# State-space layer of a decoder step: PSUM sums of prompt and samples parted, output powers formed with PSUM operands

## Chip, cores and metric

One core of one Trainium2 chip. The metric is the time of one execution on the device in microseconds (us), the median of the runs; lower is better. A program is also executed once under the hardware profiler, and all rows below come from that execution.

## What is computed

A step of a two-layer decoder on 1024 prompt tokens and 8 x 4 sample tokens, width 1024, all in float32. Only the first half of layer 0 matters here, a diagonal state-space layer (S5): 64 groups of 16 channels, each group driving 64 complex states.

```
ab = exp(dt*a)                       (complex, per group and state)
bu = einsum('blgc,gnc->blgn', u, bb) (u: normed input; bb: input matrix)
x[l] = ab*x[l-1] + bu[l]             (prompt from 0, samples from a given state)
y = Re(einsum('blgn,gcn->blgc', x, c)) + d*u
out = glu(gelu(y) @ w_glu);  also returned: the last x of prompt and samples
```

A GLU, an MLP, the shared K/V projection and layer 1 (window attention and MLP) follow. They are large matmuls and the change doesn't touch them.

## The kernel before

The method `ssm` works the state-space layer off in eight **parts** (`ft`) of 8 groups, 128 channels. Tokens are taken 8 at a time: 128 blocks of the prompt, and 8 columns for the samples. For a part:

- `s1_p` (GpSimd) forms input powers, `s1_PT` transposes them on TensorE; `s1_u` scales the input (ScalarE), `s1_U` transposes it into `U`, 136 columns used as sums: 128 prompt blocks and 8 samples. `s1_e` (GpSimd) forms the rotation table `E`.
- `s1_q` (VectorE, lines 500 to 511) forms the output powers `Q` = powers of ab times C: six instructions of 128 x 512 elements, four multiplies (L508, L509), then L510 and L511. `ap9` holds the powers of ab, `Cq` holds C, `dt0` and `dt1` are work space; all of them in SBUF. GpSimd's complex multiplies run through L409 to L414.
- `s2_S` (L551): 16 matmuls of 136 columns sum blocks into the PSUM tile `b_s`, prompt and samples together, four banks; ScalarE copies the sample columns out (L560).
- `s2_rot` (VectorE): part 0 turns the sums (L577 to L579), part 1 runs eight scans (L570), turns back and writes the states `H_` (L572 to L574). All of it reads or writes `b_s` in place.
- `s1_K` (TensorE, L533) forms the short convolution kernel in a PSUM bank, `s1_K2` (VectorE, L536, L537) takes it out, and a round trip through DRAM on the SP queue (`kdd`) lays it out as `T_`.
- `s3_y` (TensorE, L591, L595): the output, in two halves with `s1_K` between, then gelu (ScalarE, L597). `s3_zt` and `s3_zT` transpose it back, each group of transposes into an auxiliary bank that ScalarE copies out (L603, L607, L613, L617; also L550, L523, L527 for the other transposes).

A matmul of float32 is two or more instructions in the trace (two for each of L558's). PSUM has eight banks of 512 floats in a partition. `self.psum(aux=4,s=1)` (L622) shares them out: four auxiliary ones in rotation, and one `b_s` of four banks. A tile that is reused waits for the last user of the buffer; within a tile, too, waits go by the tile and not by its columns. Each engine works its queue off in the order of the program, and the order is the source's. One turn of the loop (`i`), with part i+1 summed, part i put out and part i+2 prepared:

```
if ok(i+1): s2_S(i+1)
if ok(i+2): s1_u(i+2)
if ok(i): s3_y(i,K)          # K is s1_K(i+1), between its halves
s2_rot(i+1,0); s1_K2(i+1); s2_h(i+1); s2_rot(i+1,1)
if ok(i+2): s1_bd(i+2); s1_q(i+2); s1_PT(i+2)
if ok(i): s3_zt(i)
if ok(i+2): s1_U(i+2)
if ok(i): s3_zT(i)
if ok(i+2): s1_e(i+2)
if ok(i+3): s1_p(i+3)
```

Behind the loop the banks are shared out anew for the GLU (`acc=3`), whose first matmuls take banks that `b_s` had.

Of the kernel before, what the change touches and what calls it, by code (L numbers as in the profile page):

```python
# [5 lines left out]
F=mybir.dt.float32; R=mybir.dt.float32r; I32=mybir.dt.int32  # L6
AF=mybir.ActivationFunctionType; OP=mybir.AluOpType
P=128; D=1024; NT=1056; NB=352; KT=8; DFF=4096; EPS=1e-6
# [38 lines left out]
class Core:  # L47
# [212 lines left out]
    def ssm(self, out_p, out_s, early):  # L260
# [6 lines left out]
        def pc(t,a,n): return t[:,a:a+n]  # L267
        v3=lambda ap,g: ap.rearrange("p (g n) -> p g n",g=g)
        E_=[pc(S[i],0,1024).rearrange("p (c g k) -> p c g k",c=2,g=4) for i in (0,1)]
        U_=[v3(pc(S[i],1024,1152),8) for i in (0,1)]  # L270
        PT_=[v3(pc(S[i],0,1024),8) for i in (2,3)]
        Q_=[pc(S[i],1024,1152).rearrange("p (c g t e) -> p c g t e",c=2,g=4,t=9) for i in (2,3)]
        T_=[[W[0][:,0:848],W[6][:,0:848]],[S[i][:,0:848] for i in (4,5)]]
        H_=pc(S[4],1024,1096).rearrange("p (c g k) -> p c g k",c=2,g=4)
        dt0=pc(S[5],1024,576); dt1=pc(S[5],1600,576)
# [10 lines left out]
        Cq=pc(rt,1024,1024).rearrange("p (c g e) -> p c g e",c=2,g=32)  # L286
# [5 lines left out]
        Shi=pc(ex,576,512).rearrange("p (c b g) -> p c b g",c=2,b=8)  # L292
# [54 lines left out]
        pb=self.bank()  # L347
# [52 lines left out]
        sn=pc(W[6],0,256).rearrange("p (j g) -> p j g",j=8); cn=pc(W[6],256,256).rearrange("p (j g) -> p j g",j=8)  # L400
# [7 lines left out]
        def cmul(eng,o,a,b,t):  # L408
            eng.tensor_tensor(o[0],a[0],b[0],op=mult)  # L409
            eng.tensor_tensor(t[0],a[1],b[1],op=mult)  # L410
            eng.tensor_tensor(o[1],a[0],b[1],op=mult)
            eng.tensor_tensor(t[1],a[1],b[0],op=mult)
            eng.tensor_tensor(o[0],o[0],t[0],op=sub)
            eng.tensor_tensor(o[1],o[1],t[1],op=add)  # L414
# [37 lines left out]
        def xs_row(i):  # L452
            PL.tensor_tensor(xsb[i].rearrange("p g (r c) -> p r g c",r=8),xst[i].rearrange("p r (g c) -> p r g c",g=8),pc(W[3],800,8).unsqueeze(2).unsqueeze(3).to_broadcast([P,8,8,16]),op=mult)
# [8 lines left out]
        pb=self.bank()  # L462
# [17 lines left out]
            A.copy(pc(ac,1536,512),pb)  # L480
        kdd=self.dp.tile([8,16,1920],F,name="kdd")
        sh=[P,4,8,16]; sh7=[P,4,7,16]
        sp={}

        def gsl(ft): return slice(4*ft,4*ft+4)
        def s1_u(ft):
            for r in range(8):
                A.mul(uf[:,:,r,:],x_t[(7-r)//2][:,(7-r)%2,ft*128:ft*128+128].rearrange("p (g c) -> p g c",g=8),rp[:,7-r:8-r])
        def s1_p(ft,eng=PL,t=None):
            gs=gsl(ft); t=[a[:,0:448].rearrange("p (g t e) -> p g t e",g=4,t=7) for a in t or pt]  # L490
            A.copy(P_[:,:,:,0,:],Bg[:,:,gs,:])
            cmul(eng,[P_[:,0,:,1:8],P_[:,1,:,1:8]],[ap9[:,c,gs,1:8].unsqueeze(3).to_broadcast(sh7) for c in range(2)],
                 [Bg[:,c,gs,:].unsqueeze(2).to_broadcast(sh7) for c in range(2)],t)
        def s1_e(ft,eng=PL,t=None):
            gs=gsl(ft); t=[a[:,0:448].rearrange("p (g t e) -> p g t e",g=4,t=7) for a in t or pt]
            E=E_[ft%2]
            A.copy(E[:,:,:,0:16],B16[:,:,gs,:])
            cmul(eng,[E[:,c].rearrange("p g (t e) -> p g t e",e=16)[:,:,1:8] for c in range(2)],[A8[:,c,gs,1:8].unsqueeze(3).to_broadcast(sh7) for c in range(2)],
                 [B16[:,c,gs,:].unsqueeze(2).to_broadcast(sh7) for c in range(2)],t)
        def s1_q(ft):  # L500

            gs=gsl(ft); Q=Q_[ft%2]
            t0=dt0[:,0:512].rearrange("p (g t e) -> p g t e",g=4,t=8); t1=dt1[:,0:512].rearrange("p (g t e) -> p g t e",g=4,t=8)
            a=[ap9[:,c,gs,1:9].unsqueeze(3).to_broadcast(sh) for c in range(2)]
            q=[Cq[:,c,gs,:].unsqueeze(2).to_broadcast(sh) for c in range(2)]
            A.copy(Q[:,:,:,0,:],Cq[:,:,gs,:])
            q0,q1=Q[:,0,:,1:9],Q[:,1,:,1:9]
            V.tensor_tensor(q0,a[0],q[0],op=mult); V.tensor_tensor(t0,a[1],q[1],op=mult)  # L508
            V.tensor_tensor(q1,a[0],q[1],op=mult); V.tensor_tensor(t1,a[1],q[0],op=mult)  # L509
            V.tensor_tensor(q0,q0,t0,op=add)  # L510
            V.tensor_tensor(q1,q1,t1,op=sub)  # L511
# [4 lines left out]
        def s1_U(ft):  # L516
            U=U_[ft%2]
            for h in range(2):
                pb=self.bank()
                for i in range(4):  # L520
                    g=4*h+i
                    T.transpose(pb[:,i*128:i*128+128],uf[:,g,:,:],ident)
                A.copy(U[:,4*h:4*h+4,8:136],v3(pb,4))  # L523
            pb=self.bank(); p0=32*(ft%4)
            for g in range(8):
                T.transpose(pb[:,g*16:g*16+16],xsb[ft//4][p0:p0+16,g,:],ident[p0:p0+16,p0:p0+16])
            A.copy(U.rearrange("p g (a b) -> p g a b",b=8)[:,:,0:18:17,:],pb[:,0:128].rearrange("p (g a b) -> p g a b",g=8,a=2))  # L527
        kb={}
        def s1_K(ft):
            pb=kb[ft]=self.bank(); Q=Q_[ft%2]  # L530
            for gp in range(4):
                for c in range(2):
                    T.matmul(pb[32*gp:32*gp+32,0:128],Bd[ft%2][:,c,gp,:],Q[:,c,gp,0:8,:],start=c==0,stop=c==1)  # L533
# [8 lines left out]
        def s1_PT(ft):  # L542
            PT=PT_[ft%2]
            for h in range(2):
                pb=self.bank()
                pv=pb.rearrange("p (a g c n) -> p a g c n",a=2,g=2,c=2)
                for a in range(2):
                    for c in range(2):
                        T.transpose(pv[:,a,:,c,:],P_[:,c,2*h+a,:,:],ident)
                A.copy(PT[:,4*h:4*h+4,:],v3(pb,4))  # L550
        def s2_S(ft):  # L551

            PT=PT_[ft%2]; U=U_[ft%2]
            s=sp[ft]=self.pp["s"].tile([P,2,2,512],F,name="b_s",tag="b_s")
            for c in range(2):
                for gp in range(4):
                    for h in range(2):
                        T.matmul(s[64*h:64*h+64,c,gp//2,136*(gp%2):136*(gp%2)+136],PT[:,2*gp+h,64*c:64*c+64],U[:,2*gp+h,8:144],start=True,stop=True)  # L558
            for c in range(2):
                A.copy(Shi[:,c,:,gsl(ft)].rearrange("p q (b g) -> p b g q",b=2),s[:,c,:,0:272].rearrange("p b (g k) -> p b g k",g=2)[:,:,:,128:136])  # L560
        def s2_rot(ft,part):
            b4=lambda ap: ap.rearrange("p (b g) k -> p b g k",b=2)
            E=E_[ft%2]; Er,Ei=b4(E[:,0]),b4(E[:,1]); tt=V.tensor_tensor
            t0,t1=[t[:,0:512].rearrange("p (b g k) -> p b g k",b=2,g=2) for t in (dt0,dt1)]
            s=sp[ft]; Sr,Si=[s[:,c,:,0:272].rearrange("p b (g k) -> p b g k",g=2)[:,:,:,0:128] for c in range(2)]
            if part:
                for c in range(2):
                    for gp in range(4):
                        z=s[:,c,gp//2,136*(gp%2):136*(gp%2)+128]
                        V.tensor_tensor_scan(z,rho8[:,4*ft+gp:4*ft+gp+1].to_broadcast([P,128]),z,0.0,mult,add)  # L570
                Hr,Hi=[b4(H_[:,c,:,9:137]) for c in range(2)]
                tt(Hr,Sr,Er,op=mult); tt(Hi,Sr,Ei,op=mult)  # L572
                tt(Sr,Si,Ei,op=mult); tt(Si,Si,Er,op=mult)  # L573
                tt(Hr,Hr,Sr,op=sub); tt(Hi,Hi,Si,op=add)  # L574
                sp.pop(ft)
                return
            tt(t0,Si,Ei,op=mult); tt(t1,Sr,Ei,op=mult)  # L577
            tt(Sr,Sr,Er,op=mult); tt(Si,Si,Er,op=mult)
            tt(Sr,Sr,t0,op=add); tt(Si,Si,t1,op=sub)  # L579
# [39 lines left out]
        zl=self.zs=[]  # L619
        def split_z(n,eng=None):  # L620
            for k in range(len(zl),n): zl.append(self.xsplit(X[k],self.ZO[k],eng=eng))
        self.psum(aux=4,s=1)  # L622
        s1_p(0,V,[dt0,dt1]); s1_u(0); s1_q(0); s1_PT(0); s1_U(0); s1_e(0,V,[dt0,dt1]); s1_p(1); xs_row(1)
        for i in range(-1,7):
            if ok(i+1): s2_S(i+1)
# [27 lines left out]
        t=[pc(S[7],512+256*i,256).rearrange("p (b g) -> p b g",b=8) for i in range(2)]  # L653
# [566 lines left out]
```

## Time and profile before

| | |
|---|---|
| median of 3 runs (lowest, highest) | 2328.33 us (2324.35, 2329.13) |
| the profiled execution | 2328.08 us, its span 2326.3 us |
| busy: PE, PEld, DVE, ACT, POOL | 96%, 93%, 48%, 30%, 19% of the span |
| chain of work that ended last | PE 84%, DVE 11%, ACT 2%, issue 2%, POOL 1% |
| granted clock of TensorE, mean | 0.982 |

The profile names engines so: PE is TensorE's matmuls, PEld its weight loads, DVE is VectorE, ACT ScalarE, POOL GpSimd, SP the DMA queue. L157 is line 157 of the kernel. [...] The shares are means over the whole span, of which the state-space loop is less than a tenth, so they tell nothing of what binds it: that has to be read from the stretch itself.

### The profile page before, as it was taken

What the parts mean: (1) busy time and instruction counts of PE and PEld (TensorE: products, weight loads), DVE (VectorE), ACT (ScalarE), POOL (GpSimd) and SP (SyncE); (2) the same over time, 40 slices, a digit from 0 to 9 for tenths busy, and PEclk for the clock granted to TensorE, in tenths of its full rate; (3) what the DMA queues carried; (4) which work ended last, traced back from release to release, by engine and by line L of the source; (5) the groups of instructions that cost most, each with busy time, mean ns of one, the idle gap of its engine ahead of it and who ended that gap; (6) DMA issues with size and microseconds to landing.
All of it is one profiled execution on the core that took longest, in us unless ns stands there. A gap on an engine that the chain in (4) does not pass through costs nothing.

```text
span 2326.3 us, 35574 instructions
## 1 busy us (share of the span) xinstructions
PE 2231.5 (96%) x14614; PEld 2165.7 (93%) x14614; DVE 1111.9 (48%) x2271; ACT 702.7 (30%) x1496; POOL 439.0 (19%) x477
## 2 busy tenths in 40 slices
PE   4788999999999999999999899989999999999999
PEld 3667999999999999999999887779999999999998
DVE  8996232333333333333647788884333333333332
ACT  4456422211111111111447766662111111111112
POOL 7672000101001011010014444412010010110100
PEclk8889999999999999999999999999999999999999
DMA  4114111111111111111110111011111111111112
GB/s 116 44 51 105 37 37 55 37 55 45 38 55 37 46 54 38 55 46 38 46 41 27 44 46 46 19 50 43 46 46 46 46 46 46 46 46 46 46 37 75
DMA packets 157702, 111.78 MB, mean 48 GB/s; under 512 B 14916, under 2 KB 152756, under 8 KB 156932
## 3 DMA queue, kind: packets, MB, share of 16 engines
q1 hardware_dynamic: 157540, 109.51, 16.2%
q8 instruction: 115, 1.88, 0.3%
q14 instruction: 47, 0.39, 0.1%
HBM read 103.56 MB, written 7.96 MB: 48 GB/s over the span
## 4 chain that ended last, share of the span: by engine, by line
PE 84%; DVE 11%; ACT 2%; issue 2%; POOL 1%; DMA 0%; ACTq 0%; SPq 0%; DVEq 0%; POOLq 0%
PE b_acc L157 76%; PE b_acc L967 2%; DVE S L920 1%; DVE S L931 1%; DVE S L508 1%; ACT S L926 1%; DVE x L975 1%; DVE S L509 1%; PE b_aux L595 1%; PE b_aux L591 1%; DVE S L912 1%; PE b_acc L165 0%; DVE S L181 0%; PE b_sc L918 0%; DVE b_s L573 0%
## 5 line engine op out<-in xcount | busy, mean ns | idle before, releaser
L157 PE MATMUL b_acc<-S,W 128*128 128x352 f32 x11016 | 1796.8, 324 | 7.3 <-DVE S L574 4.3
L157 PEld LDWEIGHTS b_acc<-S,W 128*128 128x128 f32 x11016 | 1780.7, 188 | 9.5 <-DVE S L574 4.4
L226 POOL TENSOR_TENSOR rt<-rt 128x352 f32<-128x352 f32 x192 | 148.5, 773 | 1227.5 <-DVE rt L224 1227.5
L241 DVE TENSOR_TENSOR x<-x,b_acc 128x352 f32<-128x352 f32 x384 | 176.9, 515 | 407.9 <-PE b_acc L157 403.1
L110 ACT CAST W<-W 128x1024 fp32r<-128x1024 f32 x152 | 158.5, 1044 | 534.4 <-PE b_acc L157 443.5
L225 ACT ACTIVATE S<-rt 128x352 fp32r<-128x352 f32 x192 | 95.6, 498 | 633.1 <-DVE rt L224 633.1
L224 DVE SCALAR_TENSOR_TENSOR rt<-b_acc,rt 128x352 f32<-128x352 f32 x192 | 99.6, 519 | 345.6 <-PE b_acc L157 334.7
L111 DVE TENSOR_TENSOR W<-W,W 128x1024 fp32r<-128x1024 f32 x142 | 173.3, 1221 | 52.9 <-ACT W L110 51.2
L227 DVE TENSOR_TENSOR S<-rt,S 128x352 fp32r<-128x352 f32 x192 | 100.8, 525 | 183.1 <-POOL rt L226 183.1
L967 PE MATMUL b_acc<-oh,W 128*128 128x256 f32 (+1 forms) x768 | 117.7, 299 | 5.0 <-POOL W L111 2.0
L967 PEld LDWEIGHTS b_acc<-oh,W 128*128 128x128 f32 x768 | 101.3, 194 | 19.2 <-issue 11.5
L926 ACT ACTIVATE S<-S,small 128x257 f32<-128x257 f32 (+1 forms) x128 | 62.0, 487 | 42.6 <-DVE small L921 42.6
L196 POOL TENSOR_TENSOR small<-small,cs 128x9 f32<-128x9 f32 x3 | 5.4, 1808 | 306.9 <-DVE small L195 306.9
L931 DVE TENSOR_SCALAR S<-S,small 128x256 f32<-128x256 f32 (+1 forms) x128 | 55.7, 477 | 2.3
L948 PE MATMUL b_pv<-S,S 128*64 128x256 f32 x240 | 36.4, 403 | 15.4 <-DVE S L941 14.1
L717 DVE TENSOR_TENSOR rt<-b_acc,rt 128x352 f32<-128x352 f32 x24 | 12.4, 519 | 74.5 <-PE b_acc L157 74.5
L974 POOL TENSOR_TENSOR x<-x,W 128x256 f32<-128x256 f32 (+1 forms) x30 | 23.9, 798 | 117.6 <-ACT W L973 103.9
L920 DVE CUSTOM_DVE_ANT_0 S<-b_sc,S 128x256 f32<-128x256 f32 (+1 forms) x124 | 43.3, 401 | 2.4 <-PE b_sc L918 2.2
L186 ACT ACTIVATE accs<-x 128x1056 f32<-128x1056 f32 x17 | 18.5, 1086 | 77.5 <-DVE x L718 77.0
L975 DVE TENSOR_TENSOR x<-x,b_acc 128x256 f32<-128x256 f32 (+1 forms) x98 | 39.8, 419 | 4.0 <-PE b_acc L967 3.8
L948 PEld LDWEIGHTS b_pv<-S,S 128*64 128x64 f32 x240 | 13.0, 136 | 28.8 <-DVE S L941 21.5
L918 PE MATMUL b_sc<-S,S 128*128 128x256 f32 (+1 forms) x248 | 38.5, 301 | 0.0
(360 smaller groups left out, 1813.7 us busy)
## 6 DMA issues: line engine op xcount, KB each, us to landing
W<-in_w_up_dram SPq DMA_DIRECT2D x64, 512.0 KB
W<-in_w_down_dram SPq DMA_DIRECT2D x64, 512.0 KB
W<-in_ssm_w_glu_dram SPq DMA_DIRECT2D x16, 512.0 KB
S<-in_x_prompt_dram SPq DMA_DIRECT2D x4, 1024.0 KB
W<-in_w_q_dram SPq DMA_DIRECT2D x8, 512.0 KB
W<-in_w_o_dram SPq DMA_DIRECT2D x8, 512.0 KB
out_y_p_dram<-S SPq DMA_DIRECT2D x16, 256.0 KB
W<-kdd SPq DMA_DIRECT2D x8, 424.0 KB
```

The source lines that it names most:

```text
L110: nc.scalar.copy(hi,raw)
L111: (eng or nc.vector).tensor_tensor(lo,raw,hi.bitcast(F),op=OP.subtract)
L157: nc.tensor.matmul(ps[nb][:,:NB],wk,x[:,part,nb*NB:(nb+1)*NB], start=start and k==0 and part==0 and w is hi, stop=stop and k==K-1 and w is lo)
L224: nc.vector.scalar_tensor_tensor(t,ps[nb][:,:NB],0.0,self.rbc[:,sl],op0=OP.max,op1=OP.mult)
L225: nc.scalar.square(s[:,0,sl],t)
L226: nc.gpsimd.tensor_tensor(q,t,t,op=OP.mult)
L227: nc.vector.tensor_tensor(s[:,1,sl],q,s[:,0,sl].bitcast(F),op=OP.subtract)
L241: nc.vector.tensor_tensor(xn,xn,pss[j][nb][:,:NB],op=OP.add)
L920: V.tensor_tensor_reduce(S[:,h,k0:256],bs[h//2][:,(h%2)*256+k0:(h%2)*256+256],Z.bias[:,h,k0:256],1.0,-3e38,OP.add,OP.max,mx[:,h:h+1])
L926: A.activation(S[:,h,k0:257],S[:,h,k0:257],AF.Exp,bias=nm[:,h:h+1],accum_out=den[:,h:h+1])
L931: V.tensor_scalar(S[:,h,k0:256],S[:,h,k0:256],rd[:,h:h+1],None,op0=mult)
L967: T.matmul(pb[:,:n],wt[:,k,c0:c0+P],o[:,part,k,:],start=k==0 and part==0 and wt is hi,stop=k==1 and wt is lo)
```

## The change

The prompt's sums and the samples' sums are parted. The prompt's go to a tile of two banks, one for the real and one for the imaginary part, of which there are two in turn (`s=2`). The samples' go by 16 matmuls of their own, 8 columns each, to the first 64 columns of a new single bank `b_c` (`c=1`), from which one copy takes them out. The next 128 columns of that bank take C for the part that comes next, copied by ScalarE (after: L509), and the 128 after that the convolution kernel of `s1_K`, which had an auxiliary bank before. The auxiliary banks go from four to three. `s1_q` of parts 1 to 7 reads C from `b_c` and has the prompt sums of the part before, no longer needed then, as work space.

```diff
         gs=gsl(ft); Q=Q_[ft%2]
...
             A.copy(Q[:,:,:,0,:],Cq[:,:,gs,:])
+            if ft:
+                cq=cb[0][:,64:192].rearrange("p (c g e) -> p c g e",c=2,g=4)
+                A.copy(cq,Cq[:,:,gs,:])
+                q=[cq[:,c].unsqueeze(2).to_broadcast(sh) for c in range(2)]
+                t0,t1=[sp[ft-1][:,c,:].rearrange("p (g t e) -> p g t e",g=4,t=8) for c in range(2)]
...
         def s1_K(ft):
-            pb=kb[ft]=self.bank(); Q=Q_[ft%2]
+            pb=kb[ft]=cb[0][:,192:320]; Q=Q_[ft%2]
...
         def s2_S(ft):
             PT=PT_[ft%2]; U=U_[ft%2]
-            s=sp[ft]=self.pp["s"].tile([P,2,2,512],F,name="b_s",tag="b_s")
+            s=sp[ft]=self.pp["s"].tile([P,2,512],F,name="b_s",tag="b_s")
+            cb[0]=self.pp["c"].tile([P,512],F,name="b_c",tag="b_c")
+            sn=cb[0][:,0:64].rearrange("p (c g q) -> p c g q",c=2,g=4)
             for c in range(2):
                 for gp in range(4):
                     for h in range(2):
-                        T.matmul(s[64*h:64*h+64,c,gp//2,136*(gp%2):136*(gp%2)+136],PT[:,2*gp+h,64*c:64*c+64],U[:,2*gp+h,8:144],start=True,stop=True)
+                        T.matmul(s[64*h:64*h+64,c,128*gp:128*gp+128],PT[:,2*gp+h,64*c:64*c+64],U[:,2*gp+h,8:136],start=True,stop=True)
             for c in range(2):
-                A.copy(Shi[:,c,:,gsl(ft)].rearrange("p q (b g) -> p b g q",b=2),s[:,c,:,0:272].rearrange("p b (g k) -> p b g k",g=2)[:,:,:,128:136])
+                for gp in range(4):
+                    for h in range(2):
+                        T.matmul(sn[64*h:64*h+64,c,gp],PT[:,2*gp+h,64*c:64*c+64],U[:,2*gp+h,136:144],start=True,stop=True)
+            A.copy(Shi[:,:,:,gsl(ft)].rearrange("p c q g -> p c g q"),sn)
...
-        self.psum(aux=4,s=1)
+        self.psum(aux=3,s=2,c=1)
```

`s2_rot` has the new shape of `b_s` in its views and is otherwise the same. Three places of the engines' queues, with the waits in brackets (`DVE_49` is the signal that VectorE raises, `DMAHW` those of transfers). VectorE, from the end of `s2_rot` through `s1_q` to the next part's `s2_rot`, before (`rt` holds C, `ex` the powers of ab, S_91 the work space, b_s the sums):

```order
L574 TENSOR_TENSOR S_90<-S_90,b_s 128x4x128
L508 TENSOR_TENSOR S_88<-ex,rt 128x4x128
L508 TENSOR_TENSOR S_91<-ex,rt 128x512
L509 TENSOR_TENSOR S_88<-ex,rt 128x4x128
L509 TENSOR_TENSOR S_91<-ex,rt 128x512
L510 TENSOR_TENSOR S_88<-S_88,S_91 128x4x128 [waits DVE_49]
L511 TENSOR_TENSOR S_88<-S_88,S_91 128x4x128 [waits DVE_49]
```

and with the change:

```order
L583 TENSOR_TENSOR S_90<-S_90,b_s 128x4x128
L513 TENSOR_TENSOR S_88<-ex,b_c 128x4x128 [waits Activation_49]
L513 TENSOR_TENSOR b_s<-ex,b_c 128x512 [waits DVE_49]
L514 TENSOR_TENSOR S_88<-ex,b_c 128x4x128
L514 TENSOR_TENSOR b_s<-ex,b_c 128x512 [waits DVE_49]
L515 TENSOR_TENSOR S_88<-S_88,b_s 128x4x128 [waits DVE_49]
L516 TENSOR_TENSOR S_88<-S_88,b_s 128x4x128
```

Nothing moved; each of the six now has one input in PSUM, two write there, and the first waits for ScalarE's copy of C. TensorE, from the sums through `s3_y` with `s1_K` between its halves, before:

```order
L558 MATMUL b_s<-S_86,S_88 64x136 [waits DVE_49,Activation_49]
L558 MATMUL b_s<-S_86,S_88 64x136 x15
L591 MATMUL b_aux<-S_87,S_90 128x136 [waits DMAHW5_49,PE_49]
L591 MATMUL b_aux<-S_87,S_90 128x136 [waits Activation_49]
...
L533 MATMUL b_aux<-S_88,W_101 32x128 [waits DVE_49,Activation_49]
L533 MATMUL b_aux<-S_88,W_101 32x128 [waits DVE_49]
```

and with the change:

```order
L565 MATMUL b_s<-S_86,S_88 64x128 x16
L569 MATMUL b_c<-S_86,S_88 64x8 [waits DVE_49]
L569 MATMUL b_c<-S_86,S_88 64x8 x15
L599 MATMUL b_aux<-S_87,S_90 128x136 [waits DMAHW5_49,Activation_49]
L599 MATMUL b_aux<-S_87,S_90 128x136 [waits Activation_49]
...
L538 MATMUL b_c<-S_88,W_101 32x128 [waits DVE_49,Activation_49]
L538 MATMUL b_c<-S_88,W_101 32x128 [waits DVE_49]
```

The prompt's sums no longer wait; the samples' sums behind them wait for VectorE, which reads C in the bank. `s1_K` waits for ScalarE, too, which copies the samples' sums out of the same bank. ScalarE, ahead of the copies of transposes, before:

```order
L597 ACTIVATE S_92<-b_aux 128x2x136 [waits PE_49,Activation_49] x4
L582 COPY S_90<-accs 128x4x8 [waits Activation_49] x2
L515 COPY W_101<-rt 64x8x16 x2
L506 COPY S_88<-rt 128x8x16
L550 COPY S_88<-b_aux 128x512 [waits PE_49] x2
```

and with the change:

```order
L605 ACTIVATE S_92<-b_aux 128x2x136 [waits PE_49,Activation_49] x4
L590 COPY S_90<-accs 128x4x8 [waits Activation_49] x2
L520 COPY W_101<-rt 64x8x16 x2
L506 COPY S_88<-rt 128x8x16
L509 COPY b_c<-rt 128x128 [waits DVE_49,Activation_49]
L555 COPY S_88<-b_aux 128x512 [waits PE_49] x2
```

The copy of C is new; it waits for VectorE, which reads the convolution kernel in the same tile.

## Rows read from the trace of the kernel before

**Rows 1.** Chain of waits: start us, us, what.
```profile
269.00 154.22 PE b_acc L157 x954
...
431.06 720.83 PE b_acc L157 x4464
```

**Rows 2.** Busy time by stage: stretch, us; PE, PEld, DVE, ACT, POOL; clock, DMA.
```profile
92.00:115.00 23.00, 20.15 (x170) 16.48 (x170) 22.28 (x36) 11.04 (x34) 14.41 (x12) 0.80 0.17 44
```

**Rows 3.** Timeline of VectorE in the loop: start us, us, instructions merged.
```profile
58.57 8.43 DVE L508 TENSOR_TENSOR S<-ex,rt 128x512 f32<-128x512 f32 x2
66.92 1.28 DVE L509 TENSOR_TENSOR S<-ex,rt 128x512 f32<-128x512 f32 x2
...
101.81 2.33 DVE L508 TENSOR_TENSOR S<-ex,rt 128x512 f32<-128x512 f32 x2
104.06 2.79 DVE L509 TENSOR_TENSOR S<-ex,rt 128x512 f32<-128x512 f32 x2
106.77 1.43 DVE L510 TENSOR_TENSOR S<-S,S 128x512 f32<-128x512 f32 x1
...
109.48 1.27 DVE L577 TENSOR_TENSOR S<-b_s,S 128x512 f32<-128x512 f32 x2
...
113.47 0.22 DVE L536 SCALAR_TENSOR_TENSOR S<-cst,ex,b_aux 128x16 f32<-128x16 f32 x1
...
121.57 2.82 DVE L508 TENSOR_TENSOR S<-ex,rt 128x512 f32<-128x512 f32 x2
...
199.50 1.28 DVE L574 TENSOR_TENSOR S<-S,b_s 128x512 f32<-128x512 f32 x2
```

**Rows 4.** Timeline of GpSimd in the loop.
```profile
104.91 1.39 POOL L410 TENSOR_TENSOR S<-accs 128x448 f32<-128x448 f32 x1
...
118.42 0.95 POOL L411 TENSOR_TENSOR S<-ex,rt 128x448 f32<-128x448 f32 x1
```

**Rows 5.** VectorE's instructions on b_s, 70 to 182 us: count, ns least/median/most.
```profile
L577 DVE TENSOR_TENSOR S<-b_s,S x12: 672/676/678, 69.3 to 171.3; 128x512 f32<-128x512 f32 x12
...
L579 DVE TENSOR_TENSOR b_s<-b_s,S x12: 699/699/700, 72.0 to 174.1; 128x512 f32<-128x512 f32 x12
```

**Rows 6.** Timeline of TensorE in the loop; in brackets idle before, and releaser.
```profile
58.80 3.90 PE L558 MATMUL b_s<-S,S 128*64 128x136 f32 x32 [4.43 <-DVE S L574]
...
95.58 1.69 PE L549 MATMUL b_aux<-cst,S 128*128 128x128 f32 x8
...
98.62 1.09 PE L522 MATMUL b_aux<-cst,W 128*128 128x128 f32 x8
...
102.03 2.07 PE L558 MATMUL b_s<-S,S 128*64 128x136 f32 x32 [0.37 <-ACT x L613]
104.04 0.73 PE L591 MATMUL b_aux<-S,W 128*128 128x136 f32 x4
...
109.61 0.66 PE L533 MATMUL b_aux<-S,W 128*32 128x128 f32 x14 [0.89 <-DVE S L511]
```

**Rows 7.** Timeline of ScalarE in the loop.
```profile
65.44 1.28 ACT L597 ACT_TABLE_LOAD   x1
...
97.21 0.30 ACT L506 COPY S<-rt 128x128 f32<-128x128 f32 x1
...
99.32 0.57 ACT L607 COPY S<-b_aux 8x512 f32<-8x512 f32 x1
```

**Rows 8.** Timeline of TensorE in layer 1, narrow matmuls.
```profile
1371.16 1.10 PE L1026 MATMUL b_acc<-W,W 128*64 128x16 f32 x16
1372.20 2.89 PE L741 MATMUL b_acc<-cst,S 128*128 128x2 f32 x18
```

**Rows 9.** Busy time and granted clock in three stretches, columns as in rows 2.
```profile
102.00:110.00 8.00, 5.49 (x71) 4.50 (x72) 8.00 (x7) 4.72 (x18) 8.00 (x7) 1.00 0.16 40
110.00:118.00 8.00, 8.00 (x52) 6.63 (x44) 7.52 (x17) 3.06 (x10) 3.06 (x4) 0.57 0.07 20
...
1374.00:1380.00 6.00, 6.00 (x28) 6.00 (x28) 3.89 (x18) 1.96 (x8) 3.79 (x3) 0.50 0.56 200
```

More of the change, by code (lines that the diff above doesn't have):

```diff
@@ L482, in ssm @@
         sh=[P,4,8,16]; sh7=[P,4,7,16]
-        sp={}
+        sp={}; cb=[None]
         def gsl(ft): return slice(4*ft,4*ft+4)
@@ L557, in s2_S @@
                     for h in range(2):
-                        T.matmul(s[64*h:64*h+64,c,gp//2,136*(gp%2):136*(gp%2)+136],PT[:,2*gp+h,64*c:64*c+64],U[:,2*gp+h,8:144],start=True,stop=True)
+                        T.matmul(s[64*h:64*h+64,c,128*gp:128*gp+128],PT[:,2*gp+h,64*c:64*c+64],U[:,2*gp+h,8:136],start=True,stop=True)
             for c in range(2):
-                A.copy(Shi[:,c,:,gsl(ft)].rearrange("p q (b g) -> p b g q",b=2),s[:,c,:,0:272].rearrange("p b (g k) -> p b g k",g=2)[:,:,:,128:136])
+                for gp in range(4):
+                    for h in range(2):
+                        T.matmul(sn[64*h:64*h+64,c,gp],PT[:,2*gp+h,64*c:64*c+64],U[:,2*gp+h,136:144],start=True,stop=True)
+            A.copy(Shi[:,:,:,gsl(ft)].rearrange("p c q g -> p c g q"),sn)
         def s2_rot(ft,part):
[L562 to L565, printed above, removed]
+            E=E_[ft%2]; Er,Ei=E[:,0],E[:,1]; tt=V.tensor_tensor
+            t0,t1=[t[:,0:512].rearrange("p (g k) -> p g k",g=4) for t in (dt0,dt1)]
+            s=sp[ft]; Sr,Si=[s[:,c].rearrange("p (g k) -> p g k",g=4) for c in range(2)]
             if part:
@@ L568, in s2_rot @@
                     for gp in range(4):
-                        z=s[:,c,gp//2,136*(gp%2):136*(gp%2)+128]
+                        z=s[:,c,128*gp:128*gp+128]
                         V.tensor_tensor_scan(z,rho8[:,4*ft+gp:4*ft+gp+1].to_broadcast([P,128]),z,0.0,mult,add)
-                Hr,Hi=[b4(H_[:,c,:,9:137]) for c in range(2)]
+                Hr,Hi=[H_[:,c,:,9:137] for c in range(2)]
                 tt(Hr,Sr,Er,op=mult); tt(Hi,Sr,Ei,op=mult)
@@ L574, in s2_rot @@
                 tt(Hr,Hr,Sr,op=sub); tt(Hi,Hi,Si,op=add)
-                sp.pop(ft)
                 return
```

## The prediction

> **What bounds the kernel now.** I read the chain of waits first: behind 269 us it is TensorE almost without a gap, in stretches like the 154 and 721 us of [rows 1]; so nothing that ends the state-space layer earlier is lost behind it, and the whole change lies in the loop over the eight parts, which ends at 201 us. There the busy times by stage say VectorE: 22.28 of 23.00 us, against 20.15 for TensorE at a granted clock of 0.80 [rows 2]. The timeline of VectorE gives the beat. I count from the first instruction of `s1_q` to the next one's: from 58.57 to the end of the last `s2_rot` at 200.78 (199.50 + 1.28) there are seven beats, 142.2 us, 20.3 each; one runs from 101.81 to 121.57 [rows 3]. Of that, all but `s1_q` (109.48 to 121.57) takes 12.1 us, and `s1_q` the rest, 7.7.
>
> Why is `s1_q` that long? Its six instructions take 1.28 a pair or about 0.64 each where GpSimd rests, but 2.79 a pair and 1.43 alone where GpSimd runs [rows 3]; GpSimd's own multiplies go from 0.95 to 1.39 us meanwhile [rows 4]. In the first beat one pair took 8.43. These instructions have both inputs in SBUF. The instructions of `s2_rot`, same size, one input in PSUM, take 672 to 700 ns at all places between 70 and 182 us, least and most [rows 5], with GpSimd running beside some of them (118.42, [rows 4]). So the slow-down belongs to two SBUF inputs, and not to the output: L577 writes SBUF.
>
> **The change part by part.** *Output powers.* For parts 1 to 7 each of the six instructions now has one SBUF input. Four write SBUF and are like L577, two write PSUM and are like L579 [rows 5]. Behind each other L577 and what follows stand 0.60 to 0.72 apart; six make 3.95 us. VectorE's floor for a beat is then 12.1 + 3.95 = 16.05 against 20.3.
> [...]
>
> *C copied to PSUM by ScalarE.* One copy of 128 elements like L506, 0.30 by its row [rows 7], of which a tenth overlaps the next copy: 0.2. It waits for VectorE's reads of the convolution kernel, which come before the second half of `s3_y` and so before the gelu ahead of it in ScalarE's queue; it ends some 3 us before `s1_q` wants it. The 0.2 counts only in TensorE's loop below, since the copies of the transposes queue behind it.
>
> *Sample sums apart.* Sixteen matmuls of 8 columns, two passes each, 32 passes. No such row exists; the nearest is L1026, the same 128x64 weights with 16 columns: 16 passes in 1.04 (1371.16 to 1372.20) [rows 8], so 65 ns, and the 136-column sums take 2.01/32 = 63 ns (102.03 to 104.04) [rows 6]: the columns hardly matter. I take 2.05 us. Below: the 32-column weights of L533, 14 in 0.66, would give 1.4. Above: the half clock of 58.80, 3.9. One copy of the states replaces two, for a gain off the path.
>
> *Two buffers for the prompt sums.* They no longer wait for the end of `s2_rot` (L574). But the sample sums behind them share the one bank with C, so they wait for the fourth instruction of `s1_q`, 2.65 us into the beat, and `s3_y` is queued behind them on TensorE. Nothing on SP or GpSimd moves; the kernel's round trip through DRAM gets 3 us more time, as `s3_y` starts later behind its `s1_K2`.
>
> *Three auxiliary banks, not four.* Each group of transposes now waits for the copy three groups back. From the end of `s3_y` (95.58, where L549 starts [rows 6]) ScalarE copies without a gap: it is done with the second of the zt groups at 99.32 [rows 7], 3.75 later, 3.95 with C. The second U group needs that bank; from there to the end of the last transpose TensorE needs 2.5 (99.16, half of L522, to 101.66, where the 0.37 idle ahead of L558 begins) [rows 6]. Together 6.6 us from the end of `s3_y` to the next sums.
>
> **The new beat.** TensorE in a ring: 6.6 + sums 2.0 + sample sums 2.05 + first half of `s3_y` (four groups of 0.73, overlapping a little) 2.65 + `s1_K` 0.7 + second half 2.65 = 16.65, if the clock is full. Through both engines: 2.75 (fourth instruction and its signal) + 2.05 + 2.65 + 0.7 + 0.1, then 113.47 to 121.57 [rows 3], 8.1: 16.35. VectorE alone 16.05. I take TensorE's 16.7. VectorE then idles about half a us in a beat, ahead of L541, which waits for `s1_K`.
> First beat: the sums run early, TensorE then rests 4 us for `s1_q`, and after such a rest (4.43 us) L558 ran at half speed, 3.90 [rows 6]. So 16.35 + 1.85 = 18.2. Second: ScalarE's table load for gelu, 1.28 [rows 7], falls ahead of it and holds the second half of `s3_y` for want of a third bank: 17.9. Five more of 16.7: 83.5. Sum 119.6 against 142.2, a gain of 22.6. The last beat's end is as before: the first matmuls of the GLU wait for L574 (the banks are reused), and the weight loads stand the same distance behind it.
> The profiled execution took 2328.08, so **2305.5 us**. The median, 2328.33, is 0.25 above it, which I leave out. About 0.2% (4.7 us) is what a measurement of this kernel tells from no change.
>
> **The rivals.**
> *VectorE stays the bound.* If the sample sums cost 1.4, or TensorE does better in its tail, its ring is under 16.05 and the beat is VectorE's floor: 18.2 + 6 x 16.05 = 114.5, a gain of 27.7, 2300.4. For it: the margin is 0.6 us in a beat. Against it: the 65 ns of L1026. [...]
> *Half clock in every beat.* [...] But the sample sums are 2 us of narrow matmuls, and behind the 1.10 of L1026 and 2.89 of two-column ones [rows 8] the clock was 0.50 for 6 us, with TensorE never idle [rows 9]. If they bring the old stretch back, the beat is 16.65 + 3.4 = 20.05: 18.2 + 17.9 + 5 x 20.05 = 136.4, a gain of 5.8, 2322.3.
> *Slower.* The same mechanism, kept up: if TensorE stays at half clock through the whole beat, its ring is 3.9 (as at 58.80, [rows 6]) + twice 2.05, 2.65, 0.7 and 2.65, another 16.1, + 6.6 with its 2.5 doubled, 9.1: 29.1, and the loop 18.2 + 17.9 + 5 x 29.1 = 181.6, so 2367.5. It decides where a beat loses more than 20.3 - 16.65 = 3.65, that is from 7.3 us of half clock in a beat, against 6.9 today. Against it: with TensorE as the bound no wait as long as today's is left to start it.
> *It does not do what it says.* If the slow-down hangs on something else than the second SBUF input, the beat stays at 20.3 and the time at 2328. Against it stand all the rows of `s2_rot`.
>
> **How the numbers follow.** TensorE's ring at full clock 0.52 (its own range 2302 to 2311: a beat of 16.2 to 17.7); VectorE's floor 0.22; half clock in each beat 0.17; slower 0.05; no effect 0.04. The range takes in the first three, 2299 to 2323. Faster 0.91, same 0.04, slower 0.05.
>
> **What would show it.** Right: L513 to L516 at about 0.6 to 0.7 each beside a running GpSimd, whose multiplies stay at 0.95; the 32 passes of L569 about 2.05; a short wait ahead of L541 on TensorE; a granted clock near 1.00 from the third beat on; beats of 16.7. Wrong: VectorE without any gap (then its floor holds), 0.50 in the clock behind L569, or a wait of TensorE at L569 for `s1_q` of more than a few tenths in the later beats.

## The result, and the profile with the change

| | before | with the change |
|---|---|---|
| median of the runs (lowest, highest) | 2328.23 us (2324.35, 2329.13), 4 runs | 2297.97 us (2297.34, 2299.69), 4 runs |
| ratio to before, 95% interval | | 0.988, 0.9867 to 0.9894 |
| the profiled execution, its span | 2328.08 us, 2326.3 us | 2297.34 us, 2295.6 us |

The change makes the kernel 30 us faster, 1.2%. The forecast was 2305.5, so 7.5 us too slow, and the measured time lies 1 us below the low end of the range. Where the time comes from is read in the same order as before the change.

The chain of waits of the changed kernel, to answer [rows 1]; columns are start, us, what:

```profile
238.89 154.22 PE b_acc L157 x954
...
400.96 720.83 PE b_acc L157 x4464
```

The two long stretches of TensorE are as long as they were and start 30.11 and 30.10 us earlier (269.00 and 431.06 before). So of the 30.74 us between the two profiled executions nearly all is gained ahead of 239 us. The rest, 0.6, arises between 1254 us (where a stretch of TensorE still starts 30.11 earlier) and 1562 us (30.69 earlier); its cause was not looked for.

Busy time by stage with the change (stretch; PE, PEld, DVE, ACT, POOL with their instructions; granted clock, as a share of the full one; DMA), to answer [rows 2, 9]:

```profile
55.00:71.00 16.00, 13.51 (x132) 11.37 (x130) 13.46 (x25) 5.53 (x17) 10.88 (x12) 0.68 0.25 62
...
87.00:103.00 16.00, 15.03 (x186) 12.48 (x185) 15.36 (x29) 11.89 (x37) 11.73 (x12) 1.00 0.23 63
```

The clock is 0.68 in the first beat and 1.00 in the later one, where the stretch before the change had 0.80. VectorE is busy for 15.36 of 16 us, TensorE for 15.03: the two are now close to each other, and which of them binds must be read from the timelines.

VectorE's timeline (start, us, instructions merged; in brackets the idle time before and what ended it), to answer [rows 3]:

```profile
58.60 0.68 DVE L513 TENSOR_TENSOR S<-ex,b_c 128x512 f32<-128x512 f32 x1
...
68.58 0.23 DVE L541 SCALAR_TENSOR_TENSOR S<-cst,ex,b_c 128x16 f32<-128x16 f32 x1 [2.16 <-PE b_c L538]
...
76.69 0.68 DVE L513 TENSOR_TENSOR S<-ex,b_c 128x512 f32<-128x512 f32 x1
...
92.51 0.68 DVE L513 TENSOR_TENSOR S<-ex,b_c 128x512 f32<-128x512 f32 x1
...
95.63 0.68 DVE L516 TENSOR_TENSOR S<-S,b_s 128x512 f32<-128x512 f32 x1
96.23 1.28 DVE L585 TENSOR_TENSOR S<-b_s,S 128x512 f32<-128x512 f32 x2
...
100.23 0.22 DVE L541 SCALAR_TENSOR_TENSOR S<-cst,ex,b_c 128x16 f32<-128x16 f32 x1
...
108.33 0.68 DVE L513 TENSOR_TENSOR S<-ex,b_c 128x512 f32<-128x512 f32 x1
...
170.40 1.28 DVE L583 TENSOR_TENSOR S<-S,b_s 128x512 f32<-128x512 f32 x2
```

The beats are read from the first L513 of each `s1_q`: 18.09 (58.60 to 76.69), then 15.82 and 15.82 again (76.69, 92.51, 108.33), and so to the end, (171.68 - 76.69)/6 = 15.83 each. The loop takes 113.1 us where it took 142.2: 29.1 gained. `s1_q` takes 3.72 (92.51 to 96.23) where the beat of [rows 3] had 7.7. In the first beat VectorE waits 2.16 for `s1_K`; in a later one its row at L541 carries no bracket, nor does any other of its rows from 76.69 to the end of the loop: VectorE is the bound.

GpSimd beside that `s1_q`, to answer [rows 4], and VectorE's instructions on the new bank between 70 and 175 us (count, ns least/median/most, start of the first and last), to answer [rows 5]:

```profile
94.58 0.96 POOL L410 TENSOR_TENSOR S<-accs 128x448 f32<-128x448 f32 x1
```

```profile
L513 DVE TENSOR_TENSOR S<-ex,b_c x6: 679/679/680, 76.7 to 155.8; 128x512 f32<-128x512 f32 x6
L513 DVE TENSOR_TENSOR b_s<-ex,b_c x6: 686/689/690, 77.3 to 156.4; 128x512 f32<-128x512 f32 x6
```

GpSimd multiplies in 0.96 us beside `s1_q`, where L410 took 1.39 before, and the multiplies take 679 and 689 ns each time. Neither engine holds up the other any more.

TensorE's timeline, to answer [rows 6]:

```profile
55.12 3.62 PE L565 MATMUL b_s<-S,S 128*64 128x128 f32 x32
61.23 1.31 PE L569 MATMUL b_c<-S,S 128*64 128x8 f32 x32 [2.49 <-DVE b_s L514]
...
86.59 1.27 PE L554 MATMUL b_aux<-cst,S 128*128 128x128 f32 x8
...
89.26 0.66 PE L610 MATMUL b_aux<-cst,S 128*128 128x128 f32 x4 [0.97 <-ACT S L555]
...
93.37 1.97 PE L565 MATMUL b_s<-S,S 128*64 128x128 f32 x32
95.17 1.05 PE L569 MATMUL b_c<-S,S 128*64 128x8 f32 x32
96.16 0.73 PE L599 MATMUL b_aux<-S,W 128*128 128x136 f32 x4
...
102.05 1.27 PE L554 MATMUL b_aux<-cst,S 128*128 128x128 f32 x8
...
171.74 3.00 PE L157 MATMUL b_acc<-S,W 128*128 128x352 f32 x9 [1.88 <-DVE S L583]
174.54 0.66 PE L599 MATMUL b_aux<-S,S 128*128 128x136 f32 x4
```

One turn of TensorE's ring runs from 86.59 to 102.05, 15.46 us: 6.78 of tail, with 0.97 of waiting for an auxiliary bank in it, 1.80 for the prompt's sums (93.37 to 95.17), 0.99 for the samples' (to 96.16), then `s3_y` and `s1_K`, 5.89. This ring is 0.36 shorter than VectorE's beat, so TensorE gains on VectorE until it has to wait for it. (The end of one group overlaps the start of the next, so a term is taken from start to start.) In the last four beats it does wait: the weight loads ahead of the samples' sums stand 0.32 to 0.38 for L514, the fourth instruction of `s1_q`. One of them:

```profile
126.68 1.01 PEld L569 LDWEIGHTS b_c<-S,S 128*64 128x64 f32 x32 [0.38 <-DVE b_s L514]
```

### The profile page after: what moved, and what is told of

Read it like the earlier page. It is cut to its first block, busy times and chain, and to the rows that moved or that the text cites. A ratio compares the mean times of both kernels' runs of the same rounds, so it can differ in the third digit from the quotient of the medians.

```text
span 2295.6 us, 36054 instructions
## 1 busy us (share of the span) xinstructions
PE 2223.2 (97%) x14870; PEld 2159.2 (94%) x14870; DVE 1081.7 (47%) x2271; ACT 703.8 (31%) x1495; POOL 427.0 (19%) x477
## 4 chain that ended last, share of the span: by engine, by line
PE 83%; DVE 11%; ACT 3%; issue 1%; POOL 1%; DMA 0%; ACTq 0%; SPq 0%; DVEq 0%; POOLq 0%
PE b_acc L157 77%; DVE S L928 1%; PE b_acc L975 1%; DVE S L939 1%; ACT S L934 1%; DVE b_s L579 1%; DVE x L983 1%; DVE S L920 1%; PE b_acc L165 1%; DVE b_s L582 0%; DVE S L181 0%; DVE b_s L586 0%; DVE S L583 0%; PE b_acc L849 0%; PE b_acc L848 0%
## 5 line engine op out<-in xcount | busy, mean ns | idle before, releaser
L157 PE MATMUL b_acc<-S,W 128*128 128x352 f32 x11016 | 1795.3, 324 | 4.9 <-DVE S L583 1.9
L157 PEld LDWEIGHTS b_acc<-S,W 128*128 128x128 f32 x11016 | 1779.2, 188 | 7.1 <-DVE S L583 2.0
```

Of the source, the lines that this page charges most:

```text
L157: nc.tensor.matmul(ps[nb][:,:NB],wk,x[:,part,nb*NB:(nb+1)*NB], start=start and k==0 and part==0 and w is hi, stop=stop and k==K-1 and w is lo)
```

## The experiments

Theory A says that the gain is the operands: `s1_q` no longer meets GpSimd's reads. Theory B says that it is the order: with two buffers the prompt's sums need not wait for the end of `s2_rot`. The ratios are to the kernel before, run on the same chip.

**One buffer for the prompt's sums.**

```diff
-        self.psum(aux=3,s=2,c=1)
+        self.psum(aux=3,s=1,c=1)
```

> The changed kernel with one buffer for the prompt sums (two banks left idle), all else as changed. Theory A (operands): the beat was set by VectorE's s1_q beside GpSimd, and the change works by its operands. Then the sums wait only for the end of s1_q, 3.7 us into the beat; VectorE idles about 1.9 us ahead of s2_rot and the beat goes from 15.82 to about 18.0: 2311 to 2313 us, still well under before. Theory B (freed order): the gain comes from the sums that no longer wait for s2_rot, the operands are incidental. Then the gain is lost: about 2326.

Measured: 2332.45, ratio 1.0029 (1.0017 to 1.0042). The whole gain is gone, and a little more; neither theory had that. Its waits between 60 and 200 us (engine, line, on whom; us in total, times, longest) and a piece of TensorE's timeline:

```profile
DVE S L585 <- PE b_s L565: 24.7, 7, 4.0
PE b_s L565 <- DVE S L516: 22.2, 7, 7.4
```

```profile
102.78 2.81 PE L565 MATMUL b_s<-S,S 128*64 128x128 f32 x32 [2.70 <-DVE S L516]
...
107.14 1.27 PE L599 MATMUL b_aux<-S,W 128*128 128x136 f32 x4
```

`s1_q` stays fast. But its work space lies in the sums' tile, so with one buffer the next sums wait for L516, the last instruction of `s1_q`, and not for `s2_rot` as before the change. What ran beside `s1_q` now stands behind it, VectorE waits for it in its turn, and TensorE comes out of its wait slower (1.27 at L599, which takes 0.73 in the changed kernel at a granted clock of 1.00; over the 20 us from 90 the clock here is 0.84). Whether that came of the work space or of the three auxiliary banks was left to later runs.

**Operands back in SBUF, two buffers kept.**

```diff
-            if ft:
+            if False:
                 cq=cb[0][:,64:192].rearrange("p (c g e) -> p c g e",c=2,g=4)
```

> The changed kernel with C and the work space of s1_q in SBUF again, the banks as changed (two buffers, three auxiliary banks, samples apart). Theory A: s1_q takes 7.5 to 8.3 us again where GpSimd runs, beats of about 20: 2323 to 2328. Theory B: the gain stays, 2298 to 2302.

Measured: 2327.22, ratio 1.0003 (0.9993 to 1.0012). VectorE in it:

```profile
101.62 2.61 DVE L513 TENSOR_TENSOR S<-ex,rt 128x512 f32<-128x512 f32 x2
104.15 2.97 DVE L514 TENSOR_TENSOR S<-ex,rt 128x512 f32<-128x512 f32 x2
...
121.28 2.93 DVE L513 TENSOR_TENSOR S<-ex,rt 128x512 f32<-128x512 f32 x2
```

The pairs are back at 2.6 to 3.0 and the beat at 19.66. Two buffers and parted sums alone are worth nothing that can be measured: theory B falls as a cause of its own.

**C from PSUM, the work space back in SBUF.** The line `t0,t1=[sp[ft-1]...]` is taken out, so L512 and L513 write `dt0` and `dt1` again (the lines behind it are one lower).

```diff
-                t0,t1=[sp[ft-1][:,c,:].rearrange("p (g t e) -> p g t e",g=4,t=8) for c in range(2)]
```

> The changed kernel with C in PSUM but the work space in SBUF: the four multiplies have one SBUF input and write SBUF only, the last add and subtract have two SBUF inputs again. Theory A (two SBUF inputs meet GpSimd, outputs don't matter): multiplies 0.6 each, L513 to L514 undisturbed, the add and the subtract about 1.4 each; s1_q 5.3, beat 17.4, 2309. If the writes mattered: the multiplies slow down too, s1_q 7 or more, 2322.

Measured: 2309.09, ratio 0.9929 (0.9913 to 0.9946). VectorE in it:

```profile
95.79 1.28 DVE L512 TENSOR_TENSOR S<-ex,b_c 128x512 f32<-128x512 f32 x2
...
98.18 1.40 DVE L514 TENSOR_TENSOR S<-S,S 128x512 f32<-128x512 f32 x1
...
112.96 1.28 DVE L512 TENSOR_TENSOR S<-ex,b_c 128x512 f32<-128x512 f32 x2
```

The four multiplies have one SBUF input and write SBUF, 1.28 a pair; the two that add up have two SBUF inputs and take 1.40 and more. So it is the inputs and not the output, instruction by instruction. C alone brings 0.7% of the change's 1.2%, and a beat of 17.17. The intervals of this kernel and of the change don't meet, so the work space in PSUM is worth the other 0.5%.

**The kernel before, with GpSimd's products for parts 2 to 7 left out.**

```diff
-            cmul(eng,[P_[:,0,:,1:8],P_[:,1,:,1:8]],[ap9[:,c,gs,1:8].unsqueeze(3).to_broadcast(sh7) for c in range(2)],
+            if ft<2: cmul(eng,[P_[:,0,:,1:8],P_[:,1,:,1:8]],[ap9[:,c,gs,1:8].unsqueeze(3).to_broadcast(sh7) for c in range(2)],
...
-            cmul(eng,[E[:,c].rearrange("p g (t e) -> p g t e",e=16)[:,:,1:8] for c in range(2)],[A8[:,c,gs,1:8].unsqueeze(3).to_broadcast(sh7) for c in range(2)],
+            if ft<2: cmul(eng,[E[:,c].rearrange("p g (t e) -> p g t e",e=16)[:,:,1:8] for c in range(2)],[A8[:,c,gs,1:8].unsqueeze(3).to_broadcast(sh7) for c in range(2)],
```

> The kernel before, with GpSimd's products of the input powers and rotation tables left out from part 2 on (the parts use the old ones), so that GpSimd rests in the loop. Theory A: s1_q takes 3.65 us with both inputs in SBUF, beats of 15.8 without any of the change: 2296 to 2299. Theory B: nothing changes for VectorE's order or the banks, 2326 to 2328.

Measured: 2297.38, ratio 0.9877 (0.9862 to 0.9891), as good as the change itself. VectorE in it:

```profile
107.23 1.29 DVE L508 TENSOR_TENSOR S<-ex,rt 128x512 f32<-128x512 f32 x2
...
109.64 0.68 DVE L510 TENSOR_TENSOR S<-S,S 128x512 f32<-128x512 f32 x1
...
122.95 1.29 DVE L508 TENSOR_TENSOR S<-ex,rt 128x512 f32<-128x512 f32 x2
```

Both inputs in SBUF, and still 0.65 to 0.68 each, with one buffer and four auxiliary banks: the beat is 15.72. GpSimd's work beside it is what `s1_q` paid for, and all of it.

**The samples' sums half by half.** The loop over `h` goes outside in the 16 matmuls of the samples, so that 8 follow each other into partitions 0 to 63 and 8 into the rest, in place of taking turns.

```diff
-            for c in range(2):
-                for gp in range(4):
-                    for h in range(2):
+            for h in range(2):
+                for c in range(2):
+                    for gp in range(4):
                         T.matmul(sn[64*h:64*h+64,c,gp],PT[:,2*gp+h,64*c:64*c+64],U[:,2*gp+h,136:144],start=True,stop=True)
```

> The changed kernel with the samples' sums in another order: first the eight matmuls into partitions 0 to 63, then the eight into 64 to 127, where they alternated. Theory A (alternating halves of the columns of the array overlap, so that a pass took 31 ns and not the 65 of L1026): 32 passes take about 2.05 us, TensorE's ring goes to 16.5 and becomes the bound; beat 16.5, 2301 to 2303. Rival (eight columns cost less than sixteen): 1.0 us as now, 2298.

Measured: 2301.0, ratio 0.9897 (0.9882 to 0.9912). TensorE in it:

```profile
100.36 1.77 PE L569 MATMUL b_c<-S,S 128*64 128x8 f32 x32
102.06 0.73 PE L599 MATMUL b_aux<-S,W 128*128 128x136 f32 x4
...
116.53 1.77 PE L569 MATMUL b_c<-S,S 128*64 128x8 f32 x32
```

The same 32 passes take 1.70 (53 ns each) where they take 0.99 (31 ns) in turns. TensorE's ring is 16.17 = 15.46 + 0.71 and binds. Of the 0.71, VectorE's lead of 0.36 hides half: the beat goes from 15.82 to 16.17. (The intervals of the two kernels' times overlap, so the beat decides and not the time.) The expectation was right in kind and too high in size, 2.05 and a beat of 16.5. The run shows the two times; that halves of the array overlap is the expectation's theory of them. What is left between 53 ns and the 65 of L1026, which has 16 columns and adds up in one place, no run takes apart. The samples' sums are the term that the prediction had wrong.

**Long scans; copies moved; both.** Three kernels ask what binds the changed one. The first cuts VectorE's work: eight scans of 128 become two of 512, with a table of decays that is zero at the start of each group, filled by GpSimd in one copy more a part. The second cuts TensorE's wait for a bank: two copies of ScalarE go elsewhere in its queue. The third has both edits.

```diff
-        sp={}; cb=[None]
+        sp={}; cb=[None]; rx=[pc(S[6],512*i,512).rearrange("p (g k) -> p g k",g=4) for i in range(2)]
+        for r in rx: PL.memset(r[:,:,0:1],0.0)
...
+            PL.tensor_copy(rx[ft%2][:,:,1:128],rho8[:,gs].unsqueeze(2).to_broadcast([P,4,127]))
...
-                    for gp in range(4):
-                        z=s[:,c,128*gp:128*gp+128]
-                        V.tensor_tensor_scan(z,rho8[:,4*ft+gp:4*ft+gp+1].to_broadcast([P,128]),z,0.0,mult,add)
+                    z=s[:,c]
+                    V.tensor_tensor_scan(z,rx[ft%2].rearrange("p g k -> p (g k)"),z,0.0,mult,add)
```

```diff
-            K=lambda: s1_K(i+1) if ok(i+1) else None
+            def K():
+                if ok(i+1): s1_K(i+1)
+                if ok(i+2): s1_bd(i+2)
...
-            if ok(i+2): s1_bd(i+2); s1_q(i+2); s1_PT(i+2)
+            if ok(i+2): s1_PT(i+2); s1_q(i+2)
```

> The changed kernel with two scans of 512 elements in place of eight of 128; a table of decay factors with zeros at the starts of the blocks, built by one GpSimd copy a part, resets them. VectorE's floor falls by about 2.0 us to 13.8. Theory (VectorE binds at 15.82 with TensorE's ring of 15.45 right behind): six beats gain only 0.37 each, the first and the last part 2.0 each: 2291 to 2293. Rival (TensorE's ring is far shorter than 15.45 and gives way): 2.0 in each of eight parts, 2282.

> The changed kernel with ScalarE's queue reordered: the copies of s1_bd between the halves of s3_y, the copies of the P transposes ahead of those of s1_q. TensorE no longer waits 0.97 us at L610 for a bank. Theory (VectorE binds): TensorE's ring falls to about 14.5 and nothing is gained, 2297 to 2298.5. Rival (TensorE's ring binds): 0.9 us in each of six beats, 2292 to 2293.

> Long scans and moved copies together. Theory (two rings a third of a us apart): only both give the beat its fall, to about 14.5: 6 x 1.3 and twice 2.0 less, 2285 to 2287. Rival (something else comes next, GpSimd or ScalarE): about as with long scans alone, 2291 to 2293.

Measured: long scans 2293.54, ratio 0.9863 (0.9849 to 0.9878); copies moved 2298.58, 0.9884 (0.9868 to 0.9901), no different from the change; both 2289.21 (2288.72 to 2289.74), 0.9846 (0.9831 to 0.986). TensorE with long scans, with copies moved, and with both, in this order (the lines of the kernels with long scans are one or two higher, so L611 is L610):

```profile
101.57 0.66 PE L611 MATMUL b_aux<-cst,S 128*128 128x128 f32 x4 [0.96 <-ACT S L557]
...
117.02 0.66 PE L611 MATMUL b_aux<-cst,S 128*128 128x128 f32 x4 [0.96 <-ACT S L557]
```

```profile
110.71 1.11 PE L569 MATMUL b_c<-S,S 128*64 128x8 f32 x32 [0.71 <-DVE b_s L514]
...
114.08 1.28 PE L603 MATMUL b_aux<-S,S 64*128 64x136 f32 x8
```

```profile
100.26 1.36 PE L611 MATMUL b_aux<-cst,S 128*128 128x128 f32 x8
...
115.14 1.35 PE L611 MATMUL b_aux<-cst,S 128*128 128x128 f32 x8
```

With VectorE shorter, TensorE's ring of 15.45 (101.57 to 117.02) holds the beat. With TensorE shorter, it only waits elsewhere, some 0.72 at L569 in four of the beats, and behind one of these it runs slower (1.28 at L603 for 0.73; the granted clock is 0.91 over the 20 us from 110, and 1.00 in the other stretches from 70 to 170). With both shorter the beat is 14.88, TensorE's ring again, and not the 14.5 expected: the time is 2.2 us above the range of its theory (that of long scans alone 0.5). Both savings were smaller than forecast. The moved copies shorten the tail by 0.58 (6.20, from 99.16 to 105.36 in that kernel) and not by 0.97, in part because TensorE then waits 0.18 for another copy; the long scans save VectorE 1.3 (2.5 for 3.8, up to the next instruction) and not 2.0. So VectorE binds the changed kernel, with TensorE about a third of a us behind it in each beat. The kernel with both edits beats the change as well, 0.9846 against 0.988 with intervals that don't meet, some 8 us. (Those of long scans alone and of the change overlap a little; there the beat decides.)

**One buffer again, to find what it lost.** Two kernels have one buffer and the work space in SBUF (the line that the third experiment takes out), with three and with five auxiliary banks. The second of them is not the kernel that its expectation describes, which has the work space in PSUM; that one ran after it, as the third.

```diff
-                t0,t1=[sp[ft-1][:,c,:].rearrange("p (g t e) -> p g t e",g=4,t=8) for c in range(2)]
...
-        self.psum(aux=3,s=2,c=1)
+        self.psum(aux=3,s=1,c=1)
```

```diff
-                t0,t1=[sp[ft-1][:,c,:].rearrange("p (g t e) -> p g t e",g=4,t=8) for c in range(2)]
...
-        self.psum(aux=3,s=2,c=1)
+        self.psum(aux=5,s=1,c=1)
```

```diff
-        self.psum(aux=3,s=2,c=1)
+        self.psum(aux=5,s=1,c=1)
```

> The changed kernel with one buffer for the prompt sums and the work space back in SBUF, C alone from PSUM. Theory (the second buffer is needed because the work space lies in the sums' own tile, so that with one buffer the sums wait for the end of s1_q): the sums then wait for the end of s2_rot alone, as before the change, and not for s1_q; TensorE has 1.7 us of slack in a beat of 17.2 (15.46 against the 17.17 that C alone from PSUM gave with two buffers), and VectorE's L541 comes 9 us into the beat where s1_K can be done 7 us in, so nothing waits on VectorE and the time is that of C alone from PSUM, 2309 to 2312. Rival (two buffers are needed in their own right, because TensorE's wait for the end of s2_rot brings its half clock): the granted clock falls to about 0.6 behind the sums in each beat, TensorE loses some 3.4 us a beat and its ring, 15.46 + 3.4 + a wait of 1 to 2 us, is 20: 2320 or more.

> The changed kernel with one buffer for the prompt sums and five auxiliary banks instead of three (C and the work space in PSUM as in the change). It asks whether the 2332.45 with one buffer came from the buffer or from TensorE's tail on three banks. Theory (the work space in the sums' tile holds the next sums back until s1_q ends): five banks let the tail end earlier, but the sums still wait 2 to 3 us for the end of s1_q, so nothing is gained: 2328 to 2333. Rival (three banks are too few once the sums start late): the waits of L610 for a bank, 1 us in a beat, and those of s3_y go, TensorE's ring shortens by 1 us or more a beat: 2320 to 2325.

> The changed kernel with one buffer for the prompt sums, the work space in their tile as in the change, and five auxiliary banks instead of three. (The kernel labelled e10, which was meant for this, also had the work space back in SBUF, against what its expectation says; this one asks e10's question.) Theory (the work space in the sums' tile holds the next sums back until s1_q ends): the sums still wait 2 to 3 us for the end of s1_q and lose their clock behind it, so five banks bring little: 2327 to 2333, against the 2332.45 with three banks. Rival (the three banks made the loss): the waits of L610, 1 us in a beat, go and the time falls to 2313 or less, as in e9 and e10, which had one buffer too.

Measured: 2311.49, ratio 0.9941 (0.9924 to 0.9957), for three banks; 2309.21, 0.9933 (0.9918 to 0.9948), for five; and 2330.27, 1.0028 (1.0015 to 1.004), for five banks with the work space in the sums' tile. The first two can't be told from C alone with two buffers, 0.9929. The third can't be told from one buffer with three banks, 1.0029. TensorE and VectorE in the third:

```profile
102.20 3.68 PE L565 MATMUL b_s<-S,S 128*64 128x128 f32 x32 [3.77 <-DVE S L516]
```

```profile
98.35 0.68 DVE L513 TENSOR_TENSOR S<-ex,b_c 128x512 f32<-128x512 f32 x1
...
106.03 1.29 DVE L585 TENSOR_TENSOR S<-b_s,S 128x512 f32<-128x512 f32 x2 [3.88 <-PE b_s L565]
...
118.64 0.68 DVE L513 TENSOR_TENSOR S<-ex,b_c 128x512 f32<-128x512 f32 x1
```

With five banks the tail ends earlier, and the sums wait 3.77 for L516 where they waited 2.70. The beat is `s1_q` 3.8 to its end, a wait of 3.88 for the sums, one of 0.40 at L541 for `s1_K`, and the 12.2 of the rest of VectorE's work: 20.3 (98.35 to 118.64), as long as before the change. So the second buffer has one use here: it is the price of having the work space in the sums' tile. Without that, one buffer does.

## Why the prediction was right, and where it was not

**The operands.** Right, and the gain hangs on them: with them back in SBUF the ratio is 1.0003. `s1_q` was forecast at 3.95 and takes 3.72. One multiply takes 679 ns with C from PSUM, and one instruction with both inputs in SBUF and GpSimd at rest 0.68 us: the source in PSUM costs nothing that these rows show.

**TensorE's ring.** This is the step that failed, and the term of it is the samples' sums. The prediction took 2.05 us, from the 65 ns of L1026 [rows 8] (at a granted clock of 1.00, so not half clock), and said that "the columns hardly matter". They take 0.99. L1026 writes one half of the partitions, pass after pass; the new matmuls take turns between two halves, and with the turns taken away they cost 1.70. That the 136-column sums cost 63 ns was no second witness: they take turns too, and with 128 columns they take 56 (1.80/32), with 8 columns 31. The lower bound, 1.4 from L533 [rows 6], was not low enough either (14 passes in 0.66 make even 1.5 for 32). The other terms held: the tail 6.78 against 6.6 (its two terms, 3.95 and 2.5, add up to 6.45), though the wait for a bank, 0.97, came at the second group of `s3_zt` (L610) and not at the second one of `s1_U`, where the sum had it; the sums 1.80 against 2.0; `s3_y` and `s1_K` 5.89 against 6.0. In sum 15.46, not 16.65.

**VectorE's floor.** With the ring below it, the rival "VectorE stays the bound" came true. It was priced at 16.05 a beat and a loop of 114.5; measured are 15.82 and 113.1. The 0.23 is that of `s1_q`. Of the signs that the prediction named, the one for this rival is what the profile shows: VectorE without any gap. Long scans, copies moved and both show the bound and the distance to the next one.

**The first two beats.** The first came out at 18.09 against 18.2, though not step by step: L565 itself already ran slowly (3.62 at a granted clock of 0.53), and the wait behind it was 2.49 and not 4. So that number is in part luck. The second was forecast at 17.9, for ScalarE's table load; it is like the others, 15.82. The load, at 65.25, fell in the first beat, where TensorE didn't wait for it. The prediction's own row had it there as well: 65.44 [rows 7], in the beat that began at 58.57 [rows 3].

**The last beat.** "As before" was wrong by 1.0 us. The loop ends 29.1 us earlier, the 154 us stretch starts 30.1 earlier. Ahead of the first GLU matmul TensorE was idle for 4.33 us before the change, and the first L591 behind it took 1.11:

```profile
200.84 3.00 PE L157 MATMUL b_acc<-S,W 128*128 128x352 f32 x9 [4.33 <-DVE S L574]
203.64 1.11 PE L591 MATMUL b_aux<-S,S 128*128 128x136 f32 x4
```

Now it is 1.88, and L599 takes 0.66. From there to the next L157 it was 6.3 us (to 209.95) and is 5.2 (174.54 to 179.78), which is the 1.0. That is read from the two traces; no run tried it.

The profiled execution is 8.2 us faster than the forecast: 119.6 less 113.1 makes 6.5 (some 4.4 in the five beats forecast at 16.7, 2.1 in the second), the last beat 1.0, and 0.6 lie in what was not looked for.

**The rivals that lost.** Half clock in every beat was not to be seen in the change: the narrow matmuls don't bring it here, with a granted 1.00 in all stretches from 71 us on. The 3.4 us that this rival adds to a beat are an estimate from the stretch of 110 to 118 us [rows 9], 8 us times the 0.43 that the granted 0.57 lacks (6.9 us, if the lower clock is the 0.50 of the same rows); no run of the change shows them. Behind a wait of TensorE a lower clock was seen: once with the copies moved, and in every beat of the kernels with one buffer and the work space in PSUM, where it is 0.83 to 0.91 in each 20 us from 70 to 150. But the length of the wait doesn't settle it. Of the four waits of some 0.72 us with the copies moved, one was followed by the 0.91; with one buffer, the work space in SBUF and three banks, the sums waited 0.71 us up to 114.06 and then took 1.97, and the clock was 1.00 over the 20 us from 110. What decides is open. The kernels with one buffer also show how near the slower side lay. The prediction sought it in the clock alone and took the second buffer for a gain; it is a need.

## What to carry to other kernels

Where VectorE and GpSimd both read SBUF, look at the two inputs of VectorE's instructions before cutting any work: C in PSUM, by one short copy on ScalarE for each part, was worth 0.7% here, and the work space in PSUM another 0.5%. A tile that is borrowed as work space lives longer, so count who waits for its next use; it may need a second buffer that it did not need before. And a matmul's price is taken from a row with the same pattern of output partitions, not only of the same size (31 or 53 ns a pass here).

## What was not expected of the hardware

- Small float32 matmuls with 128x64 weights and 8 columns cost 31 ns a pass when they take turns between the two halves of the partitions, and 53 when they don't, though a single one is listed with the same median, 203 ns, in both kernels.
- The engine that is held up can be held up for long. In the kernel with one buffer, the work space in SBUF and three banks, one instruction of VectorE with two SBUF inputs took 3.70 us (the same line took 0.68 to 5.44 over the seven beats), and GpSimd went on beside it undisturbed, at 0.94 and 1.12 us where the kernel before has 0.95 and 1.15 ahead of `s1_q` (97.25 to 102.04):

```profile
116.31 3.70 DVE L514 TENSOR_TENSOR S<-S,S 128x512 f32<-128x512 f32 x1
```

```profile
116.34 0.94 POOL L412 TENSOR_TENSOR S<-accs 128x448 f32<-128x448 f32 x1
117.24 1.12 POOL L413 TENSOR_TENSOR S<-S,S 128x448 f32<-128x448 f32 x1
118.33 1.12 POOL L414 TENSOR_TENSOR S<-S,S 128x448 f32<-128x448 f32 x1
```

  It ended half a us after GpSimd's last instruction did, behind three more of them and not one. What decides how long it takes, no run takes apart.
